# The list scheduler counts one microsecond instead of a quarter between another engine's work and the TensorE instruction that reads it

## The chip, the cores and the metric

The kernel runs on one core of a Trainium2 chip. The metric is the device time of one execution in microseconds, taken as the median of several runs. The core has five instruction streams: PE (TensorE, the matrix engine; PEld is its weight load), DVE (VectorE), ACT (ScalarE), POOL (GpSimd) and SP (SyncE, which here only issues DMAs). Each works off its own list of instructions in the order in which the program gives them; semaphores make an instruction wait for one of another engine.

## The reference

The computation is a network of four layers on 256 tokens of width 1024. The first two layers (`hybrid_layer`) normalise the residual, project it by one wide matrix, and run three branches whose results are gated and added:

```python
h = rms_norm(x, norm_w)
proj = h @ w_in                                   # 1024 -> 14352
y_a = diff_attention_branch(...)                  # 8 heads, softmax minus lambda * softmax
y_c = conformer_conv_branch(...)                  # 31-tap depthwise convolution, layer norm
y_d = gated_deltanet_branch(...)                  # chunked delta rule, triangular solve
return x + (g_a * y_a + g_c * y_c + g_d * y_d) @ w_out
```

Two more layers (`second_block`) follow. Each has a normalisation modulated by a condition vector, attention with two key/value heads, a hyena branch (a long convolution by FFT, whose filter is made by a small network of sines), a merge by gates, and a SwiGLU feed-forward part. In the third layer these run on two sequences (the 256 tokens and a context of 256); in the fourth on the tokens alone, with the context giving only keys and values. A final norm ends it. All is float32.

## The kernel before, in words

Tokens lie along the free dimension in most stages, features along the 128 partitions. A product of float32 accuracy is made of three passes: each operand is split into a high part (a copy by ACT to a narrower matmul type) and a low part (DVE subtracts the high part from the original), and `mm3` issues high times high, high times low and low times high as one unit into the same PSUM tile. Weights go the same way: `piece` lets SP load `raw` (128 x 1024 numbers, 512 KB), ACT makes `wh`, DVE makes `wl`; there are five places for `raw` and six each for `wh` and `wl`. Products of the large matrices go to three PSUM places called `gemm`; all other TensorE results share five PSUM places. Every SBUF tile called a temporary here lives in one of 54 places of 512 columns.

Between the products, DVE, ACT and POOL empty PSUM, compute softmax, convolutions, the delta rule and the splits of the activations. A norm is a chain across engines: squares on ACT, their sum on POOL or DVE (`sq`), a product with ones on PE (`ps_rms`), DVE (`rms`), a power on POOL, a diagonal matrix on DVE (`diag`), a product on PE that spreads it over the tokens (`ps_bc`), the scaled activations and their split (`h2h`, `h2l`), and only then the next products. In the third and fourth layer the hyena branch is another such chain: `vtokh` and `vtokl` (split), `ps_V` (PE), `V`, `yr` and `ys`, `Z`, `Zh` and `Zl` (split), `ps_hy` (PE). The modulation vectors (`mod_t`, 640 DVE instructions) depend on nothing but loads and are filled in wherever DVE has room.

Nothing of this is issued in program order. Every call is recorded as an `Op` (line 52) with an engine, a cost from formulas in `cost` (line 161), and edges to the operations whose results it reads or overwrites, which `touch` (line 212) finds. An edge carries a delay: `LATENCY = 0.25` us (line 42) across engines, `SAME` or nothing within one. `order` (line 329) then alternates a forward pass, a list scheduler that gives every engine the ready operation with the earliest `latest` time, and a backward pass, which works out those `latest` times from the end. It does so seven times and keeps the order whose planned span is the shortest. `emit` issues that order; the planned times themselves are thrown away. The real waits are semaphores between instructions and know nothing of the plan's delays. An operation that takes a place in SBUF or PSUM waits, in the plan, for the place to be free: that delay (lines 438 and 282) is `LATENCY` and lies outside the edges of `touch`.

An `mm3` is one operation for the plan, so that its earliest start is set by the later of its high and low operands. Since all instructions are issued from one line (472), the profile's rows are told apart by the names of their tiles.

Of the kernel before, what the change touches and what calls it, by code (L numbers as in the profile page):

```python
# [36 lines left out]
PE, DVE, ACT, POOL, DMA = range(5)  # L37
# [2 lines left out]
LATE = 0.5  # L40
HORIZON = 70.0
LATENCY = 0.25
SAME = 0.06
PASSES = 7

# [105 lines left out]
class Plan:  # L151
# [60 lines left out]
    def touch(self, op, ap, write):  # L212
        r = self.room(ap)
        if r.last is not op:
            if r.first is None:
                r.first = op
            elif r.slots:
                op.after.setdefault(r.first, -1e9)
            r.last = op
            r.touches += 1  # L220
            op.rooms.append(r)
        full = ap.full if isinstance(ap, View) else ap
        pattern = list(full.ap)
        if r.psum:
            part = (0, 1, 0, 1)
        elif full.space == DRAM:
            part = (full.offset, full.offset + 1 + sum(s * (c - 1) for s, c in pattern), 0, 1)
        else:
            p, lo = divmod(full.offset, pattern[0][0])
            part = (lo, lo + 1 + sum(s * (c - 1) for s, c in pattern[1:]), p, p + pattern[0][1])  # L230
        lo, hi, p0, p1 = part
        for wrote, accesses in ((True, r.writes), (False, r.reads)):
            if not (wrote or write):
                continue
            for o, a in accesses:
                if o is not op and a[0] < hi and lo < a[1] and a[2] < p1 and p0 < a[3]:
                    if o.engine != op.engine:
                        late = LATENCY
                    else:
                        late = SAME if wrote and not write and op.engine != PE else 0.0  # L240
                    op.after[o] = max(op.after.get(o, -1e9), late)
        if write:
            covered = lambda o, a: o is not op and lo <= a[0] and a[1] <= hi and p0 <= a[2] and a[3] <= p1
            r.writes = [x for x in r.writes if not covered(*x)]
            r.reads = [x for x in r.reads if not covered(*x)]
        (r.writes if write else r.reads).append((op, part))
# [23 lines left out]
    def backward(self, found):  # L270
# [5 lines left out]
        for op in found:  # L276
            for r in op.firsts:
                key = (id(r.slots), r.index)
                if key in last:
                    for o, _ in last[key].reads + last[key].writes:  # L280
                        if o is not op:
                            o.follow.setdefault(op, LATENCY)
                last[key] = r
# [70 lines left out]
    def forward(self):  # L354
# [28 lines left out]
        while len(found) < len(ops):  # L383
# [48 lines left out]
            for r in op.rooms:  # L432
# [3 lines left out]
                if not r.left:  # L436
                    s = r.slots
                    heappush(s.free, (op.end + LATENCY, r.index))
                    s.load[r.since:r.last.place + 1] -= 1
# [1472 lines left out]
```

## Time and profile before

| | |
|---|---|
| median of three runs | 2269.54 us (2269.27 to 2270.68) |
| the profiled execution | 2267.71 us |
| its span on the core | 2265.9 us |
| PE busy | 2222.6 us (98%), 16280 matmuls |
| DVE busy | 1912.5 us (84%) |
| ACT busy | 1114.3 us (49%) |
| POOL busy | 277.3 us (12%) |
| mean granted TensorE clock | 0.994 |

The span runs from the first to the last instruction of the program; the 1.8 us between it and the execution's time lie around it. "Busy" for PE counts the time in which at least one matmul is in the pipeline; a matmul's record lasts longer than the distance to the next one, so a waiting time shows as idle only once the pipeline has run empty.

### The profile page before, as it was taken

The page shows a single profiled execution, that of the slowest core. Times are in us where ns is not written, and L with a number is a line of the kernel's source. Part 1 is how long each engine was busy: PE and PEld are TensorE (multiplying, and loading weights), DVE is VectorE, ACT ScalarE, POOL GpSimd, SP SyncE. Part 2 cuts the span into 40 slices and gives each one's busy share as a digit, 9 for nine tenths or more (in the row PEclk, how much of TensorE's full clock was granted, in tenths as well). Part 3 has the DMA queues.
Part 4 walks back from the last instruction along what each step waited for, and adds up shares of the span by engine and source line. Part 5 has one row for each costly group of instructions (what it writes and reads, how often), then busy time and mean ns, then how long its engine had stood idle before and what let it go on. Part 6 is the DMA issues. An engine that isn't in the chain of part 4 may idle for free. (4 is left out here: it accounts for less than half of the span.)

```text
span 2265.9 us, 42914 instructions
## 1 busy us (share of the span) xinstructions
PE 2222.6 (98%) x16280; PEld 2085.7 (92%) x16280; DVE 1912.5 (84%) x4646; ACT 1114.3 (49%) x2070; POOL 277.3 (12%) x212
## 2 busy tenths in 40 slices
PE   8999999999999999999999999999999999999998
PEld 7999999999999999999889888988888898999998
DVE  8999998999999999999899988986664399867564
ACT  6556565654656665654356433332232265545443
POOL 1132110201222110111031000100000103101001
PEclk9999999999999999999999999999999999999999
DMA  7444444775545445674312566566662441555563
GB/s 267 152 150 146 129 145 161 247 242 179 168 140 142 134 143 170 232 256 139 101 57 91 155 198 206 171 203 203 212 208 77 139 145 55 170 167 196 165 197 96
DMA packets 161638, 371.14 MB, mean 164 GB/s; under 512 B 38932, under 2 KB 52500, under 8 KB 161432
## 3 DMA queue, kind: packets, MB, share of 16 engines
q1 hardware_dynamic: 161432, 368.41, 51.1%
q8 instruction: 128, 2.10, 0.4%
q14 instruction: 78, 0.64, 0.1%
HBM read 357.07 MB, written 11.28 MB: 163 GB/s over the span
## 5 line engine op out<-in xcount | busy, mean ns | idle before, releaser
L472 ACT CAST wh<-raw 128x1024 fp32r<-128x1024 f32 (+2 forms) x552 | 558.7, 1017 | 477.4 <-PE gemm L472 324.9
L472 DVE TENSOR_TENSOR wl<-raw,wh 128x1024 fp32r<-128x1024 f32 (+2 forms) x552 | 658.6, 1199 | 100.9 <-ACT wh L472 99.4
L472 PE MATMUL gemm<-hh,wh 128*128 128x256 f32 x1408 | 411.2, 292 | 0.1
L472 PE MATMUL gemm<-h2h,wh 128*128 128x256 f32 (+1 forms) x1232 | 405.1, 329 | 1.1 <-ACT h2h L472 1.1
L472 PE MATMUL gemm<-h2l,wh 128*128 128x256 f32 (+1 forms) x1232 | 401.9, 326 | 1.0 <-DVE h2l L472 0.9
L472 PE MATMUL gemm<-h2h,wl 128*128 128x256 f32 (+1 forms) x1232 | 400.8, 325 | 0.0
L472 PE MATMUL gemm<-hh,wl 128*128 128x256 f32 x1408 | 396.2, 281 | 1.4 <-DVE wl L472 1.4
L472 PE MATMUL gemm<-hl,wh 128*128 128x256 f32 x1408 | 396.5, 282 | 0.0
L472 PEld LDWEIGHTS gemm<-hh,wh 128*128 128x128 f32 x1408 | 266.5, 189 | 3.8 <-issue 2.3
L472 PEld LDWEIGHTS gemm<-hh,wl 128*128 128x128 f32 x1408 | 266.0, 189 | 2.0 <-DVE wl L472 1.8
L472 PEld LDWEIGHTS gemm<-hl,wh 128*128 128x128 f32 x1408 | 266.1, 189 | 0.1
L472 DVE CUSTOM_DVE_ANT_0 mod_t<-mod_w,mod_c 128x256 f32<-128x256 f32 x640 | 248.1, 434 | 14.1 <-DMA mod_w<-w_mod 13.8
L472 PEld LDWEIGHTS gemm<-h2h,wh 128*128 128x128 f32 x1232 | 233.0, 189 | 22.2 <-ACT h2h L472 1.2
L472 PEld LDWEIGHTS gemm<-h2l,wh 128*128 128x128 f32 x1232 | 233.1, 189 | 21.8 <-DVE h2l L472 1.6
L472 PEld LDWEIGHTS gemm<-h2h,wl 128*128 128x128 f32 x1232 | 233.3, 189 | 21.1
L472 DVE SCALAR_TENSOR_TENSOR cacc<-cu,c_conv_w,cacc 128x246 f32<-128x246 f32 (+26 forms) x480 | 228.4, 511 | 0.1
L472 POOL TENSOR_TENSOR sq<-sq 128x512 f32<-128x512 f32 (+1 forms) x39 | 56.9, 1469 | 935.9 <-ACT sq L472 934.7
L472 PE MATMUL gemm<-fh,wh 128*128 128x256 f32 (+1 forms) x374 | 123.1, 329 | 0.0
L472 PE MATMUL gemm<-fl,wh 128*128 128x256 f32 (+1 forms) x374 | 122.6, 328 | 0.0
L472 PE MATMUL gemm<-fh,wl 128*128 128x256 f32 (+1 forms) x374 | 122.5, 328 | 0.0
L472 PE MATMUL gemm<-wh,hh 128*128 128x256 f32 x320 | 93.9, 293 | 2.9 <-DVE az L472 2.4
L472 PE MATMUL gemm<-wh,h2h 128*128 128x256 f32 x320 | 93.1, 291 | 0.7 <-DVE v2l L472 0.7
(449 smaller groups left out, 5035.4 us busy)
## 6 DMA issues: line engine op xcount, KB each, us to landing
raw<-w_in SPq DMA_DIRECT2D x296, 512.0 KB, 3.7
mod_w<-w_mod SPq DMA_DIRECT2D x192, 256.0 KB, 3.5
raw<-w_gate_up SPq DMA_DIRECT2D x88, 512.0 KB, 3.7
raw<-w_out SPq DMA_DIRECT2D x32, 512.0 KB, 4.4
raw<-w_down SPq DMA_DIRECT2D x32, 384.0 KB, 3.2
raw<-w_down SPq DMA_DIRECT2D x32, 320.0 KB, 2.9
raw<-w_attn_out SPq DMA_DIRECT2D x16, 512.0 KB, 4.4
raw<-w_dn_out SPq DMA_DIRECT2D x16, 512.0 KB, 3.5
```

The costliest lines, as they stand in the source:

```text
L472: call(*map(real, args), **{k: real(x) for k, x in kw.items()})
```

## The change

Edges that lead from another engine's operation to a TensorE operation get a delay of 1.0 us in the plan instead of 0.25. This holds wherever `touch` makes the edge, so for every matmul, transpose and `mm3` that reads what DVE, ACT, POOL or a DMA wrote, and in both passes. Edges from PE to other engines, among other engines, and the turns of places in SBUF and PSUM keep 0.25. No instruction is added, removed or changed; which order each engine's list is in, and which of the free places a tile gets, is worked out anew.

```diff
 LATENCY = 0.25
+MARGIN = 1.0
 SAME = 0.06
...
                     if o.engine != op.engine:
-                        late = LATENCY
+
+                        late = MARGIN if op.engine == PE else LATENCY
                     else:
                         late = SAME if wrote and not write and op.engine != PE else 0.0
                     op.after[o] = max(op.after.get(o, -1e9), late)
```

## Rows read from the trace of the kernel before

**Rows 1.** The page's first part: busy time, share of the span, instructions.

```profile
PE 2222.6 (98%) x16280; PEld 2085.7 (92%) x16280; DVE 1912.5 (84%) x4646; ACT 1114.3 (49%) x2070; POOL 277.3 (12%) x212
```

**Rows 2.** Stretches: length, each engine's busy time (instructions), granted clock, DMA share, GB/s.

```profile
0.00:50.00 50.00, 38.84 (x304) 38.07 (x305) 41.76 (x99) 32.94 (x53) 8.62 (x15) 1.00 0.81 273
...
700.00:750.00 50.00, 47.18 (x397) 45.55 (x397) 48.30 (x120) 30.36 (x66) 16.64 (x12) 1.00 0.42 120
2000.00:2050.00 50.00, 50.00 (x425) 50.00 (x424) 30.31 (x38) 23.13 (x27) 0.00 (x0) 1.00 0.54 179
2250.00:2265.90 15.90, 6.46 (x52) 6.02 (x50) 3.97 (x9) 3.65 (x8) 4.01 (x4) 0.78 0.19 66
```

**Rows 3.** PE's waits: who waited for whom, us, times, longest.

```profile
PE gemm L472 <- ACT w4h L472: 7.1, 1, 7.1
PE gemm L472 <- DVE w4l L472: 4.1, 2, 2.5
PE ps_hy L472 <- DVE Zl L472: 3.1, 3, 1.9
PE ps_V L472 <- DVE vtokl L472: 3.1, 2, 2.4
PE gemm L472 <- DVE wl L472: 2.9, 4, 1.2
PE gemm L472 <- DVE az L472: 2.4, 2, 2.1
PE ps_rms L472 <- POOL sq L472: 2.3, 2, 1.5
PE ps_rms L472 <- DVE sq L472: 1.9, 2, 1.0
PE ps_bc L472 <- DVE diag L472: 1.5, 2, 1.4
PE ps_kk L472 <- DVE dk L472: 1.3, 1, 1.3
PE gemm L472 <- ACT h2h L472: 1.1, 1, 1.1
PE gemm L472 <- DVE h2l L472: 0.9, 2, 0.6
PE ps_rms L472 <- ACT sq L472: 0.7, 2, 0.5
PE gemm L472 <- DVE v2l L472: 0.7, 1, 0.7
PE gemm L472 <- DVE cu L472: 0.5, 1, 0.5
```

**Rows 4.** PE's timeline around the longest wait of the middle.

```profile
1153.62 0.39 PE L472 MATMUL ps_V<-vtokh,dfth 128*128 128x512 f32 x1
1156.40 0.79 PE L472 MATMUL ps_V<-vtokl,dfth 128*128 128x512 f32 x1 [2.40 <-DVE vtokl L472]
...
1160.60 0.28 PE L472 MATMUL gemm<-wh,h2h 128*128 128x256 f32 x1
```

**Rows 5.** DVE's timeline in the same stretch.

```profile
1154.53 1.21 DVE L472 TENSOR_TENSOR wl<-raw,wh 128x1024 fp32r<-128x1024 f32 x1
1155.67 1.27 DVE L472 TENSOR_TENSOR vtokl<-ps_vtok,vtokh 128x512 fp32r<-128x512 f32 x2
```

**Rows 6.** The middle's four stretches of low granted clock, columns as in rows 2.

```profile
1023.20:1033.40 10.20, 9.20 (x43) 9.20 (x44) 10.13 (x31) 4.82 (x12) 3.33 (x2) 0.50 0.58 158
1156.30:1159.70 3.40, 3.30 (x8) 2.62 (x9) 3.26 (x9) 0.99 (x2) 1.01 (x1) 0.51 0.64 204
1903.90:1907.30 3.40, 3.40 (x15) 3.11 (x15) 3.40 (x10) 0.61 (x2) 2.26 (x2) 0.50 0.00 0
2064.30:2067.70 3.40, 3.40 (x19) 3.40 (x18) 1.71 (x3) 1.04 (x1) 1.36 (x2) 0.50 0.70 255
```

**Rows 7.** The norms' chains: one row of the view of the tile ps_rms.

```profile
L472 DVE TENSOR_SCALAR rms<-ps_rms x12: 145/152/160, 18.1 to 2256.5; 128x2 f32<-128x2 f32 x12
```

## The prediction, made before the changed kernel was run

> **What bounds the kernel now.** I read the page's busy shares first, then busy time by stretches, then PE's waits, then the timelines on both sides of the longest waits, then the clock.
>
> PE is busy 2222.6 of 2265.9 us [rows 1]; 43.3 us of the span are idle PE. In a stretch of nothing but products of 256 columns PE does 425 matmuls in 50 us, 0.118 us each, with no idle time at all [rows 2]. No change of order makes that faster, so what can be won is idle time and the clock lost beside it. The first stretch of 50 us has 11.2 us of idle PE and the last 15.9 us have 9.4 [rows 2]: at the start PE waits for the first loads and their split, at the end for the last norm and the stores. In both nothing else is there to be done. That leaves 43.3 - 20.6 = 22.7 us in the middle.
>
> The waits of PE by releaser tell what these are [rows 3]. The view has 32 waits with 35.3 us in all; behind `cu` four rows of one wait each are left out (`p`, `a_sm` and `hn_y` with 0.5 us each, `d_r` with 0.2). The start's are `w4h` and `w4l` (11.2 us), the end's are `ACT sq` (0.7) and the longest one of `diag` (1.4). The remainder is 22.0 us in 26 waits, which agrees with the 22.7.
>
> They are of two kinds. `az`, `cu` and `v2l` empty a `gemm` place of PSUM: a product waited for the place, 3.6 us in 4 waits. The plan's delay for that isn't touched. The other 22 waits, 18.4 us, are for an operand made by DVE, ACT or POOL: the kind that the change is about. Nearly all are DVE's. DVE was not idle then but busy with other things: before the longest one PE issued the first product of `vtokh` at 1153.62 and got `vtokl` only for 1156.40, while DVE did a `wl` at 1154.53 and began the two `vtokl` at 1155.67 [rows 4, 5]. Products whose operands need nothing of this stood behind in PE's list (`gemm` at 1160.60). In 700 to 750 us DVE is busy 48.3 of 50 us and PE loses 2.8 [rows 2]: the order there is a matter of tenths of a microsecond on both engines.
>
> The second loss is the clock. In four stretches of the middle the granted clock is 0.5, 1.2 in place of 2.4 GHz, 20.4 us in all [rows 6]. Three begin during or just after waits (two for `POOL sq`, 2.3 us together; `vtokl` 2.4; `Zl` 1.9), the fourth without a listed wait. Fully at work, a slow stretch loses half its length: 5.1 us for the long one, 1.7 for each short one.
>
> **The change, part by part.** It adds, removes and resizes no instruction; so the direct cost is nothing, and each engine's busy time stays. Everything comes by way of the order.
>
> *PE's order.* In the plan a matmul may now start 0.75 us later after its operand than before. Where another product is ready, the scheduler puts it first. On the chip that is six products of 0.118 us between the time at which the plan takes the operand as done and the time at which PE comes to it. The semaphore wait itself is no longer: an operand that comes late by less than 0.75 us is then met without idle time, one that comes later stalls PE 0.75 us less. So a wait can lose at most its own length or 0.75 us. Row by row of the operand waits, the lesser of the row's sum and 0.75 us times its count: `Zl` 2.25, `vtokl` 1.5, `wl` 2.9, `POOL sq` 1.5, `DVE sq` 1.5, `diag` 0.1 (the one of the middle), `dk` 0.75, `h2h` 0.75, `h2l` 0.9, `p`, `a_sm` and `hn_y` 1.5, `d_r` 0.2: 13.85 us [rows 3].
>
> Of this `POOL sq` (1.5) and `h2h` (0.75) I take as nothing: they lie where one layer's norm ends and the next layer's first products need it, and there is no other product to put in between. 11.6 us are left. I take two thirds, 7.7 us. Not all, since a plan that is worked out anew brings new close meetings elsewhere; not a third, since six products' room is more than most of these waits are long (18.4 us by 22 is 0.84 us in the mean). The bounds are 0 and 18.4 us, the latter where DVE's order changes as well.
>
> *The producers' order.* The backward pass counts the same delay, so whatever feeds PE is due 0.75 us earlier. On DVE and ACT it passes by what doesn't (`mod_t`, the convolutions). The `wl` ahead of `vtokl` [rows 5] feeds PE as well, so among those two nothing changes. What empties PSUM falls back by 0.75 us against a `wl`; waits of that kind are 3.6 us now. A `wl` of 1.21 us ahead of such an instruction costs PE at most that, and with three `gemm` places mostly nothing. I take zero for this part, between -3 us (three of the longest waits end one `wl` earlier) and +3.6 (the waits for places double).
>
> *The chains.* Where PE waits in the plan anyway, the plan now shows 0.75 us of room before PE's step, and the next step on DVE or ACT is planned 0.75 us later. Into that room the scheduler can put a filler, which on the chip then delays the real step. There are 12 chains of norms [rows 7] and the double one at the seam to the third layer, 13 in all, with three steps into PE each (`ps_rms`, `ps_bc`, the first product): 39 steps. Cover is the rest of PE's work: it hides a later step wherever products are ready. It is missing where PE already waits with nothing else to do: `POOL sq` twice and `h2h` once [rows 3]. I count 3 x 0.75 = 2.25 us of loss there; the bounds are 0 and 39 x 0.75 = 29.3 us.
>
> *The clock.* Of the short slow stretches behind `vtokl` and `Zl` I count one as gone, 1.7 us: their waits of 2.4 and 1.9 us get shorter by 0.75 at most, not to nothing. The bounds are 8.5 us won (5.1 + 2 x 1.7) and as much lost, if new waits do the same elsewhere. The Trainium skill ("TensorE: Matmul & The Clock Gate", section "Why this matters for your kernels") says that idle gaps of PE between bursts of matmuls send it back to the slow clock. By that, ending the gaps would give back all three stretches; the fourth of them here stands after one-column products and no listed wait [rows 6], so the rule doesn't tell all.
>
> *Sum.* -7.7 + 0 + 2.25 - 1.7 = -7.15 us. The profiled execution took 2267.71 us (span 2265.9 and 1.8 around it), so 2260.6; the median of the runs stands 1.83 us above it, so the prediction is 2262.4, rounded 2262.
>
> **The rivals.**
>
> A. *The waits only move.* Where DVE is nearly full [rows 2], PE must wait somewhere for what DVE hasn't done; after each stall PE meets DVE with the new order's next close spot. For it: DVE busy 48.3 of 50 us while PE loses 2.8. Against it: most of the waiting time (`Zl`, `vtokl`, `sq`, `h2h`) lies in stretches where ready products stand behind. It gives between no change and a third of 11.6 us: about 2268. The Trainium skill ("Perfetto Trace Analysis", section "Optimization Strategy") has one find the gaps of the most contended engine and make the dependencies that end them start sooner or complete faster. This change does neither by itself; by that reading it stays at 2269.5.
>
> B. *The chains stretch, and it is slower.* Fillers get into the room before half of the 39 steps: 19.5 x 0.75 = 14.6 us, against 7.7 + 1.7 won: +5.2 us, 2275. It decides from 13 paid steps on (9.4 / 0.75 = 12.5), and from 19 on it is slower by more than can be told from no change. For it: the norm of the seam to the third layer already stalls PE twice within 3 us and costs 10.2 us of slow clock [rows 3, 6]. Against it: outside of five waits of norms PE has work at all of them.
>
> C. *Stalls and slow clock go together.* The order on DVE improves too, 13.85 us of waits and the two short slow stretches (3.4) go, and 2.25 for the uncovered steps stay: -15.0 us, and with the seam's slow stretch gone (-5.1) -20.1: 2249 to 2255.
>
> **How the numbers follow.** A measurement of this kernel can tell about 0.2%, 4.5 us, from no change. The forecast (2255 to 2265) has 0.43, A (2265 to 2274) 0.25, B (above 2274) 0.22, C (below 2255) 0.10. Faster is the forecast and C, 0.53; slower is B; the same is A. The range for 8 in 10 runs from 2250, which takes in most of C, to 2277, a little beyond B's middle; that leaves out a few hundredths of C and half of B. The likeliest case's own range is 2255 to 2265.
>
> **What would show it.** Right: the same counts and durations of every group; PE's waits of the middle for operands at 11 us or less in place of 18.4, above all `wl`, `DVE sq`, `Zl` and `vtokl` shorter; the waits for `az`, `cu`, `v2l` about as now; one slow stretch of the clock fewer; start and end unchanged within 1 us. A would show equal idle time under other names. B would show waits of `ps_rms`, `ps_bc`, `h2h`, `ps_V` and `ps_hy` longer, with DVE or ACT doing something unrelated just before. C would show a mean clock of 0.998 or more. The prediction is wrong if the order changes so much (another of the seven passes kept, places of SBUF taken otherwise) that the rows of before say little of the stalls of after.

## The result and the profile after

The changed kernel is slower: 2284.8 us (2282.95 to 2285.27, four runs) against 2269.4 us (2268.29 to 2270.68), a ratio of 1.0065 with a 95% interval of 1.0053 to 1.0077. The forecast was 2262 with a range up to 2277, so the sign is wrong and the range is missed by 8 us. Executions of one kernel differ too: the seven of margin_024, the widest below, lie between 2272.93 and 2283.51. The profiled execution took 2282.95 us with a span of 2280.9, which is 15.0 more than before.

The page's first part, in the columns of [rows 1], for the changed kernel:

```profile
PE 2229.4 (98%) x16280; PEld 2090.7 (92%) x16280; DVE 1919.6 (84%) x4646; ACT 1117.6 (49%) x2072; POOL 289.4 (13%) x212
```

The work is the same: the same counts on PE, DVE and POOL. PE's idle time rose from 43.3 us [rows 1] to 2280.9 - 2229.4 = 51.5. The stretches that answer to [rows 2], the third one 15 us later:

```profile
0.00:50.00 50.00, 39.53 (x306) 38.87 (x307) 40.66 (x100) 34.48 (x54) 9.78 (x15) 1.00 0.80 275
...
2015.00:2065.00 50.00, 50.00 (x424) 50.00 (x424) 30.08 (x38) 23.47 (x29) 0.00 (x0) 1.00 0.54 177
2265.00:2280.90 15.90, 6.95 (x52) 6.40 (x50) 3.98 (x9) 3.65 (x8) 4.00 (x4) 0.75 0.19 66
```

Start and end are as before within 1 us (10.5 and 9.0 us of idle PE against 11.2 and 9.4), and the stretch of mere products is still full. The loss is in the middle. PE's waits by releaser, as in [rows 3]:

```profile
PE gemm L474 <- ACT w4h L474: 7.1, 1, 7.1
PE ps_hy L474 <- DVE Zl L474: 5.0, 3, 2.8
PE gemm L474 <- DVE wl L474: 4.8, 4, 2.7
PE gemm L474 <- ACT h2h L474: 4.0, 3, 2.1
PE gemm L474 <- DVE h2l L474: 3.5, 4, 1.4
...
PE ps_rms L474 <- POOL sq L474: 2.8, 2, 1.8
PE ps_mean L474 <- POOL ln_s L474: 1.7, 2, 1.1
PE ps_bc L474 <- DVE diag L474: 1.6, 2, 1.4
...
PE ps_hyt L474 <- DVE vtokl L474: 0.8, 1, 0.8
```

With the rows left out the view has 39 waits of 44.3 us in all; before it had 32 of 35.3. Without the start (`w4h`, `w4l`, 10.5) and the end (`ACT sq` and the longest of `diag`, 2.1), and without the waits for a PSUM place (`az`, `cu`, `qk_y`, 2.0 together), 30 waits of 29.7 us for an operand remain, where 22 of 18.4 us stood before. `vtokl`, `dk` and `DVE sq` did shrink, by 4.9 us together. `Zl` and `wl` grew by 3.8, `h2h` and `h2l` by 5.5 (2.0 to 7.5), and names that had no wait before (`ln_s`, `ro_a`, `gpl`, `ycl`, `d_S` and three smaller ones) brought 7.0.

The stretches of the middle at the lower granted clock, in the columns of [rows 6]:

```profile
279.50:282.90 3.40, 3.40 (x21) 3.06 (x20) 1.65 (x4) 0.02 (x1) 0.00 (x0) 0.50 0.53 166
655.00:658.40 3.40, 3.40 (x18) 3.40 (x17) 3.40 (x6) 1.94 (x3) 0.00 (x0) 0.50 0.33 94
740.30:743.70 3.40, 3.40 (x19) 3.40 (x18) 3.40 (x10) 0.77 (x2) 3.33 (x3) 0.50 0.47 157
1033.90:1044.10 10.20, 10.20 (x48) 10.20 (x49) 4.66 (x22) 1.46 (x4) 1.51 (x2) 0.50 0.71 220
1832.60:1839.40 6.80, 5.96 (x26) 5.66 (x27) 6.80 (x18) 3.54 (x8) 0.00 (x0) 0.50 0.22 73
2085.20:2088.60 3.40, 3.32 (x15) 3.32 (x16) 3.40 (x10) 2.01 (x5) 0.00 (x0) 0.50 0.47 184
```

That is 30.6 us at 1.2 GHz where 20.4 stood before [rows 6]; at half speed it costs 5.1 us more. That is an upper figure: in the stretch at 1832.6 the products stand 0.21 us apart in place of 0.12, by which 10.2 us cost 4.6. The account of the 15.0: operand waits +11.3, waits for places -1.6, start -0.7, clock +5.1, together 14.1; 0.9 is not assigned (1.4 with the smaller figure).

**Where along the run.** The tile views give the first and last start of a stage's products. Of the changed kernel, for the merge of the first two layers (`mh`), that of the last two (`m2h`) and the feed-forward output (`fh`):

```profile
L474 PE MATMUL gemm<-mh,wh x128: 277/282/365, 496.6 to 1027.7; 128*128 128x256 f32 x128
L474 PE MATMUL gemm<-m2h,wh x160: 276/282/402, 1409.2 to 2071.2; 128*128 128x256 f32 x128, 128*128 128x512 f32 x32
L474 PE MATMUL gemm<-fh,wh x374: 274/283/401, 1594.4 to 2268.5; 128*128 128x256 f32 x110, 128*128 128x512 f32 x77
```

And of the kernel before:

```profile
L472 PE MATMUL gemm<-mh,wh x128: 277/282/288, 490.8 to 1020.0; 128*128 128x256 f32 x128
L472 PE MATMUL gemm<-m2h,wh x160: 274/282/398, 1403.3 to 2057.5; 128*128 128x256 f32 x128, 128*128 128x512 f32 x32
L472 PE MATMUL gemm<-fh,wh x374: 274/283/401, 1584.8 to 2253.5; 128*128 128x256 f32 x110, 128*128 128x512 f32 x77
```

By the last `mh` product, the end of the second layer, the new order is 1027.7 - 1020.0 = 7.7 us late; I call this the head. From the first `m2h` product (merge of the third layer) to the last `fh` product (end of the fourth) it takes 859.3 us against 850.2: 9.1 more, the tail. Between the two it wins 1.8. Of the tail's 9.1, the waits for `h2h` and `h2l` (2.0 to 7.5, all of them at three norms there) are 5.5 and the clock 1.7 (slow stretches of 10.2 us where 6.8 stood); 1.9 is not assigned.

**What happened in the tail.** PE's timeline at the norm ahead of the fourth layer, before (18 `fh` and `fl` products and `ps_f` between its rows are left out):

```profile
1817.82 0.61 PE L472 MATMUL ps_bc<-diag,ones 128*128 128x128 f32 x4
...
1821.16 0.28 PE L472 MATMUL gemm<-h2h,wh 128*128 128x256 f32 x1
```

After:

```profile
1829.62 0.28 PE L474 MATMUL gemm<-fh,wl 128*128 128x256 f32 x1
1829.73 0.60 PE L474 MATMUL ps_bc<-diag,ones 128*128 128x128 f32 x4
1830.27 0.64 PE L474 MATMUL ps_f<-f_h,c_f_w 64*64 64x256 f32 x2
1832.54 0.58 PE L474 MATMUL gemm<-h2h,wh 128*128 128x256 f32 x1 [1.62 <-ACT h2h L474]
1833.96 0.58 PE L474 MATMUL gemm<-h2l,wh 128*128 128x256 f32 x1 [0.84 <-DVE h2l L474]
```

And DVE in the same stretch, after:

```profile
1827.73 0.48 DVE L474 TENSOR_SCALAR diag<-c_ident,rms 128x128 f32<-128x128 f32 x2
...
1830.34 1.22 DVE L474 TENSOR_TENSOR wl<-raw,wh 128x1024 fp32r<-128x1024 f32 x1
1831.47 2.04 DVE L474 SCALAR_TENSOR_TENSOR h<-xres,modvFalse,ps_bc 128x256 f32<-128x256 f32 x5
```

In the kernel before, DVE in that stretch:

```profile
1817.34 0.48 DVE L472 TENSOR_SCALAR diag<-c_ident,rms 128x128 f32<-128x128 f32 x2 [0.60 <-POOL rms L472]
...
1817.94 1.21 DVE L472 TENSOR_TENSOR wl<-raw,wh 128x1024 fp32r<-128x1024 f32 x1
1819.07 1.64 DVE L472 SCALAR_TENSOR_TENSOR h<-xres,modvFalse,ps_bc 128x256 f32<-128x256 f32 x4
```

Read them together. After, `diag` is done at 1828.2, but PE first takes 13 more ready products and comes to `ps_bc` at 1829.73. Before, `ps_bc` followed `diag` at once, and 18 ready products stood *behind* it: these covered the 3.3 us in which DVE and ACT made `h2h`, although DVE put a `wl` in front of `h` then too. Now all of them stand *ahead* of `ps_bc`, behind it only two small `ps_f` are left to do, and the same `wl` is no longer hidden. PE waits 1.62 and 0.84, together 2.46 us, and from 1832.6 works at 1.2 GHz for 6.8. I call the ready products between the first `ps_bc` and the first `h2h` product the cover. At the feed-forward norm of the fourth layer the cover went from 9 products to none in the same way; here the `wl` ahead of `h` is new. The wait there went from 1.13 us to 2.74; before, then after:

```profile
2070.76 0.38 PE L472 MATMUL gemm<-h2h,wh 128*128 128x256 f32 x1 [1.13 <-ACT h2h L472]
```

```profile
2084.25 0.38 PE L474 MATMUL gemm<-h2h,wh 128*128 128x256 f32 x1 [2.09 <-ACT h2h L474]
2085.28 0.58 PE L474 MATMUL gemm<-h2l,wh 128*128 128x256 f32 x1 [0.65 <-DVE h2l L474]
```

At the third norm of the tail, the feed-forward norm of the third layer, the cover only shrank, from 30 products to 21, and the waits rose from 0.6 us to 2.3.

### The profile page after: what moved, and what is told of

Its sections match the earlier page's. It is cut to its first block, busy times and chain, and to the rows that moved or that the text cites. A ratio compares the mean times of both kernels' runs of the same rounds, so it can differ in the third digit from the quotient of the medians.

```text
span 2280.9 us, 42952 instructions
## 1 busy us (share of the span) xinstructions
PE 2229.4 (98%) x16280; PEld 2090.7 (92%) x16280; DVE 1919.6 (84%) x4646; ACT 1117.6 (49%) x2072; POOL 289.4 (13%) x212
## 5 line engine op out<-in xcount | busy, mean ns | idle before, releaser
L474 DVE CUSTOM_DVE_ANT_0 mod_t<-mod_w,mod_c 128x256 f32<-128x256 f32 x640 | 248.6, 432 | 12.8 <-DMA mod_w<-w_mod 12.1
L474 DVE SCALAR_TENSOR_TENSOR cacc<-cu,c_conv_w,cacc 128x235 f32<-128x235 f32 (+28 forms) x480 | 228.6, 516 | 0.0
```

Of the source, the lines that this page charges most:

```text
L474: call(*map(real, args), **{k: real(x) for k, x in kw.items()})
```

## The experiments

All are the changed kernel with one edit, so only the order differs; every kernel computes the whole. Two theories were to be told apart: that the longer delay on operands itself does the harm, at the norms above all, or that any new order of this scheduler costs about as much. Where an expectation speaks of "up to 997 us" and "behind 1443 us", it reads head and tail at the first `mh` product of the second layer and near the end of the third layer's `m2h`; that differs from the marks above by at most 2.0 us. The table has all runs. Clock is the time lost to the lower clock, over the three stages, summed from the granted clock in stretches of 3 us. Cover is given for the norm ahead of the fourth layer and for its feed-forward norm, counted in PE's timeline. Each ratio is to executions of the kernel before that were taken beside the run (medians 2269.4 to 2270.4). The order, and with it the cover, is the same in every execution of a kernel; head, tail, waits and clock are of the one execution that was profiled, so differences of a few microseconds between two rows show little by themselves.

| kernel | us | ratio to before, 95% | head | tail | waits `h2h`+`h2l` | cover | clock |
|---|---|---|---|---|---|---|---|
| before | 2269.4 | 1 | 0 | 0 | 2.0 | 18, 9 | 10.2 |
| after (1.0 us) | 2284.8 | 1.0065, 1.0053 to 1.0077 | +7.7 | +9.1 | 7.5 | 0, 0 | 15.3 |
| margin_024 | 2280.96 | 1.0038, 1.0024 to 1.0052 | +8.9 | +3.0 | 1.9 | 18, 9 | 25.6 |
| margin_026 | 2273.75 | 1.0019, 1.0011 to 1.0028 | +9.3 | -0.9 | 2.2 | 18, 9 | 13.6 |
| same_055 | 2277.21 | 1.0032, 1.0020 to 1.0044 | +10.0 | +1.3 | 2.7 | 15, 9 | 17.0 |
| same_065 | 2268.85 | 0.9996, 0.9987 to 1.0006 | +2.0 | +0.2 | 2.0 | 18, 9 | 11.9 |
| horizon_72 | 2276.84 | 1.0029, 1.0018 to 1.0040 | +7.4 | +2.7 | 1.9 | 18, 9 | 18.7 |
| weights_only | 2275.64 | 1.0027, 1.0017 to 1.0036 | +2.6 | +1.0 | 1.9 | 18, 9 | 10.2 |
| weights_095 | 2283.07 | 1.0055, 1.0039 to 1.0072 | +12.1 | +4.6 | 1.9 | 18, 9 | 13.6 |
| chains_only | 2280.64 | 1.0043, 1.0028 to 1.0058 | +9.5 | +5.6 | 6.8 | 0, 0 | 11.9 |
| chains_095 | 2280.79 | 1.0041, 1.0026 to 1.0056 | +12.1 | +3.8 | 3.9 | 0, 0 | 15.3 |
| norms_only | 2288.05 | 1.0074, 1.0062 to 1.0087 | +15.5 | +3.5 | 5.5 | 3, 0 | 8.5 |
| norms_quarter | 2280.25 | 1.0048, 1.0034 to 1.0062 | +14.0 | +0.3 | 2.5 | 18, 0 | 10.2 |
| diag_quarter | 2282.49 | 1.0050, 1.0030 to 1.0070 | +16.4 | +3.0 | 3.3 | 0, 12 | 18.7 |
| h2_quarter | 2276.29 | 1.0026, 1.0016 to 1.0037 | +9.4 | +7.7 | 5.9 | 0, 0 | 18.7 |
| margin_050 | 2274.79 | 1.0025, 1.0015 to 1.0034 | +8.2 | +8.0 | 6.0 | 0, 6 | 15.3 |
| margin_095 | 2279.81 | 1.0050, 1.0035 to 1.0065 | +20.8 | +3.0 | 3.7 | 0, 0 | 23.9 |
| margin_200 | 2307.47 | 1.0161, 1.0144 to 1.0178 | +26.5 | +17.5 | 11.7 | 0, 0 | 27.3 |

**Orders drawn anew.** Five kernels hardly change the delay, or leave it at 0.25 and move another constant of the plan by a little, so that the scheduler comes to another order for a reason that has next to nothing to do with operands of PE.

```diff
-MARGIN = 1.0
+MARGIN = 0.26
```

> The change with a delay of 0.26 us in place of 1.0: next to no margin, but a plan worked out from other numbers. 'Cover used up': no loss that has to do with the delay, ratio 0.998 to 1.002. 'New draw': it may lie as far off as the change itself, 0.994 to 1.008, which then is the size of the draw.

```diff
-MARGIN = 1.0
+MARGIN = 0.24
```

> The change with a delay of 0.24 us, a hundredth less than before. 'New draw' (the order before was a better than usual one, and any other set of numbers falls back): slower than before by 0.1 to 0.6%, most of it in the first two layers, like the 0.26 us (ratio 1.0019). 'Cover used up' alone: no loss, 0.999 to 1.001.

```diff
-HORIZON = 70.0
+HORIZON = 72.0
 LATENCY = 0.25
-MARGIN = 1.0
+MARGIN = 0.25
```

In same_065 and same_055 `HORIZON` stays 70.0, `MARGIN` is 0.25 as well, and `SAME` is 0.065 or 0.055 in place of 0.06.

> All delays 0.25 us as before; of the scheduler, the stretch in which buffers are given out ahead is 72 us in place of 70, which means nothing for the order of single steps but sets it anew. 'New draw': slower than before by 0.1 to 0.5%, in the first two layers (4 us or more up to 997 us of the kernel before), and next to nothing behind 1443 us. 'Change alone' (the loss of the first layers belongs to the longer delay): 0.999 to 1.001, as before.

> All delays across engines 0.25 us as before; the delay within one engine is 0.065 us in place of 0.06. The same bet as the one before: 'new draw' 1.001 to 1.005 with the loss in the first two layers, 'change alone' 0.999 to 1.001.

> All delays across engines 0.25 us, the delay within one engine 0.055 us in place of 0.06: a fifth order without a longer delay. Both theories: 0 to 9 us lost up to 997 us, 3 us or less behind 1443 us, ratio 0.999 to 1.004.

They give 0.9996, 1.0019, 1.0029, 1.0032 and 1.0038, in the mean 1.0023, about 5 us. That is within what 'new draw' had expected of all but same_065 (1.001 to 1.005). None is faster than the kernel before beyond the interval; its order is a better draw than four of these and equal to the fifth. Most of the loss is in the head (+2.0 to +10.0 us). The tail stays between -0.9 and +3.0, the waits for `h2h` and `h2l` at 1.9 to 2.7 us, and the cover at 15 or 18 and 9. So the changed kernel's +7.7 in the head is nothing that a new order alone doesn't give; its +9.1 in the tail, and the lost cover, are beyond all five.

**The delay's size.**

```diff
-MARGIN = 1.0
+MARGIN = 0.5     # 0.95 in margin_095, 2.0 in margin_200
```

> Delay 0.5 us. 'Cover used up': a third of the way from 0.26 to 1.0, ratio 1.002 to 1.004, waits for h2h and h2l of 3 to 5 us. 'New draw': no order in the delays, 0.998 to 1.010.

> Delay 0.95 us, for all that the delay means the same as 1.0. 'Cover used up': the loss behind the norms of the third and fourth layer (8.6 us between 1443 us of the kernel before and the end) is there again, 6 us or more, and the whole ratio 1.005 to 1.008. 'New draw': that part of the loss is as likely to be gone, ratio 0.998 to 1.010.

> Delay 2.0 us. 'Cover used up': the loss grows with the delay, over 12 us from 1443 us on, waits for h2h and h2l of 8 us or more, ratio 1.008 to 1.015; the waits for wl go under 1 us. 'New draw': no more than the others, 1.001 to 1.008.

At 0.5 us the tail loses 8.0 us already (in the slowest of that kernel's ten executions), at 2.0 us 17.5, with the cover of the norm ahead of the fourth layer gone in all. The waits for `h2h` and `h2l`, expected at 3 to 5 us for 0.5, are 6.0. The waits for `wl`, expected under 1 us at 2.0, are 3.1. With 0.95 us the tail lost 3.0 only: a miss for a loss that grows with the delay. DVE's timeline at that norm tells why, of margin_095:

```profile
1836.03 0.88 DVE L474 SCALAR_TENSOR_TENSOR xres<-gemm,modvTrue,xres 128x256 f32<-128x256 f32 x2 [1.71 <-PE gemm L474]
1836.83 1.65 DVE L474 SCALAR_TENSOR_TENSOR h<-xres,modvFalse,ps_bc 128x256 f32<-128x256 f32 x4
```

The first row ends a wait of DVE of 1.71 us; no `wl` stands between `ps_bc` (issued at 1835.83) and `h`. PE's wait for `h2h` is 1.01 us in place of 1.62. The longest delay is the other end; PE, of margin_200, and then DVE:

```profile
1852.08 0.71 PE L474 MATMUL ps_bc<-diag,ones 128*128 128x128 f32 x4
1856.19 0.38 PE L474 MATMUL gemm<-h2h,wh 128*128 128x256 f32 x1 [3.40 <-ACT h2h L474]
```

```profile
1852.41 1.22 DVE L474 TENSOR_TENSOR wl<-raw,wh 128x1024 fp32r<-128x1024 f32 x1
...
1854.00 1.21 DVE L474 TENSOR_TENSOR wl<-raw,wh 128x1024 fp32r<-128x1024 f32 x1
1855.13 1.64 DVE L474 SCALAR_TENSOR_TENSOR h<-xres,modvFalse,ps_bc 128x256 f32<-128x256 f32 x4
```

Two `wl` ahead of `h`, and 3.40 us. With no cover the wait for `h2h` at this norm is thus 1.0 us without a filler (the same in chains_095 and diag_quarter), 1.6 with one `wl` behind `ps_bc` (the same in margin_050 and chains_only) and 3.4 with two. The fillers fall in front of `h` or not by the draw, so the loss of one such kernel is no clean function of the delay. With cover a `wl` at the same place costs nothing: the kernel before and norms_quarter, below, have one too and don't wait for `h2h` there.

**Weights alone, and all but the weights.**

```diff
-                        late = MARGIN if op.engine == PE else LATENCY
+                        late = MARGIN if op.engine == PE and r.name in ("wh", "wl") else LATENCY
```

> The delay of 1.0 us on the split weights wh and wl alone; all chains keep 0.25. 'Cover used up': chains are not set back, so no loss at the norms, and the waits for wl (2.9 us before, 4.8 after the change) go down to 1 or 2: ratio 0.997 to 1.001. A third theory, 'weights crowd out chains' (weights get due 0.75 us earlier on DVE, so a wl of 1.2 us goes ahead of the chain's step, as at 1830 us in the changed kernel): waits for h2h and h2l of 6 us or more here too, ratio 1.003 to 1.007. 'New draw': 0.994 to 1.010.

The same with `MARGIN = 0.95`:

> 0.95 us on wh and wl alone, 0.25 on the rest. 'The delay costs on the chains only': up to 997 us it loses what an order drawn anew loses, 0 to 9 us (1.0 us on the weights lost 2.6), behind 1443 us nothing; ratio 0.999 to 1.004, waits for wl under 1 us. 'The draw alone': the same. 'Any longer delay costs': 10 us or more up to 997 us.

```diff
-                        late = MARGIN if op.engine == PE else LATENCY
+                        late = MARGIN if op.engine == PE and r.name not in ("wh", "wl") else LATENCY
```

> 1.0 us on everything but wh and wl. 'The delay costs on the chains only': 10 us or more lost up to 997 us and 3 us or more behind 1443 us, ratio 1.005 to 1.012. 'The draw alone': 0 to 9 us up to 997 us, and behind it as the change, ratio 1.002 to 1.008.

The same with `MARGIN = 0.95`:

> 0.95 us on everything but wh and wl: the same bets as for 1.0 us, drawn once more.

With the delay on the weights alone there is little waiting for `wl`: 2.9 us before, no row of that name in weights_only, 0.5 in weights_095. That the delay does this isn't shown: same_055, without a longer delay, has 0.2, and the changed kernel and norms_quarter, with 1.0 us on the weights, have 4.8 and 4.4. The cover stays (18, 9). But neither is faster. weights_only was expected at 1.001 at most if only the chains cost, weights_095 at 1.004 at most under both theories; both are above. PE's waits in weights_only show where it waits instead; the first rows without those of the start:

```profile
PE ps_hy L474 <- DVE Zl L474: 4.6, 3, 2.3
PE ps_vn L474 <- DVE d_r L474: 3.2, 4, 2.0
...
PE ps_kk L474 <- DVE dk L474: 2.8, 3, 1.0
```

`d_r` had 0.2 us before and `dk` 1.3 [rows 3], and all waits of this kernel sum to 38.6 us against 35.3. The wait stands under other names; its sum is no more than in the five draws (34.0 to 39.1). The two weights kernels differ by 0.05 us of delay and by 9.5 us in the head, which looks like a difference of draws; weights_095 alone would fit 'any longer delay costs' (10 us or more), weights_only with +2.6 speaks against it. With the delay on all but the weights the cover is gone (0, 0) and the waits for `h2h` and `h2l` are 6.8 and 3.9 us. So the lost cover and the waits behind it come by the chains, not by the weights. The tail's time doesn't part the two as cleanly: weights_095 loses 4.6 there with the cover whole, 3.4 of it by slow stretches of the clock, chains_095 3.8. The ratios of chains_only and chains_095 lie below the 1.005 that was expected if the chains alone cost.

**The norms' edges.** The names of the steps of a norm, and of the `gph` and `gpl` split, are taken out of the longer delay, or get it alone:

```diff
-                        late = MARGIN if op.engine == PE else LATENCY
+                        late = MARGIN if op.engine == PE and r.name not in ("sq", "ln_s", "diag", "h2h", "h2l", "hh", "hl", "gph", "gpl") else LATENCY
```

> The change, but the operands of the norm chains (sq, ln_s, diag, and the activations h2h, h2l, hh, hl, gph, gpl that come out of a norm) keep the delay of 0.25 us. Theory 'cover used up' (with the longer delay PE takes the ready products ahead of the norm's own step, and has none left for the wait behind it): the waits for h2h and h2l, 7.5 us after the change against 2.0 before, go back to about 2, the slow stretch of 6.8 us at 1832 us goes, and some 9 of the 15 us come back: ratio to the kernel before 1.001 to 1.004. Theory 'new draw' (any small shift of the plan throws the order of the close meetings anew): the ratio is anywhere from 0.996 to 1.010, and the waits come back under other names.

The same list with `in` for `not in`:

> The kernel before, with 1.0 us on the operands of the norm chains alone. 'Cover used up': the loss of these chains stands here by itself, waits for h2h and h2l of 6 us or more, ratio 1.003 to 1.006. 'New draw': no tie between the edges that got the longer delay and the waits that grow; ratio anywhere from 0.996 to 1.010.

With the nine names back at 0.25 the tail is at +0.3 and the waits for `h2h` and `h2l` at 2.5 us. PE of norms_quarter, the 18 products after `ps_bc` and the one of `ps_f` left out:

```profile
1829.40 0.60 PE L474 MATMUL ps_bc<-diag,ones 128*128 128x128 f32 x4
...
1832.61 0.38 PE L474 MATMUL gemm<-h2h,wh 128*128 128x256 f32 x1
```

The cover is there again, and no wait for `h2h`. The ratio, 1.0048, misses the 1.001 to 1.004 that was expected, by the head. Two things limit this reading. The feed-forward norm of the fourth layer still has no cover in this kernel; it waits less because no `wl` stands ahead of `h` (0.44 us for `h2h` in place of 2.09). And it has no slow stretch of the clock in the tail, where the kernel before loses 3.4 us; without that luck its tail would be at about +3.7. The delay on the nine names alone brings the waits (5.5 us) and takes the cover (3, 0), though the tail is only 3.5 longer; expected were 6 us or more of waits and a ratio of at most 1.006. The head is worse in both (+14.0, +15.5) than in the five draws (at most +10.0), with the delay on these names and with it off them.

**Which step of the norm.**

```diff
-                        late = MARGIN if op.engine == PE else LATENCY
+                        late = MARGIN if op.engine == PE and r.name not in ("sq", "ln_s", "diag") else LATENCY
```

> The change, with 0.25 us on what feeds the small products of a norm alone (sq, ln_s, diag); h2h, h2l and the other activations keep 1.0. 'Cover used up' puts the loss at the step of ps_bc, which PE comes to only behind the last ready products: with that step early again the waits for h2h and h2l are 3 us or less and the part behind 1443 us loses 3 us at most (8.6 in the change). If the loss sits at the activations, that part loses 6 us or more. The first two layers: a draw, 4 to 14 us lost.

The same with `("h2h", "h2l")`:

> The change, with 0.25 us on h2h and h2l alone; sq, ln_s and diag keep 1.0. 'Cover used up' at ps_bc: waits for h2h and h2l stay at 5 us or more, the part behind 1443 us loses 5 us or more. If the loss sits at the activations: 3 us or less for both. The first two layers: a draw, 4 to 14 us lost.

Taking the delay off the last step alone changes nothing: tail +7.7, waits 5.9, cover 0, 0. Taking it off the small steps alone (`sq`, `ln_s`, `diag`) brings the waits to 3.3 and the tail to +3.0, but by the timelines this is half a cure: 12 products of `gph` cover the feed-forward norm again, while ahead of the fourth layer the cover is still 0, with 1.01 us for `h2h` since no `wl` stands ahead of `h`. No single step holds the effect.

**Cover, stall and clock over all kernels.** Nine of the kernels have 0 to 3 products of cover at the norm ahead of the fourth layer, and there PE waits 1.0 to 3.4 us for `h2h`; the other nine, the kernel before among them, have 15 or 18 and don't wait for `h2h` there. In seven of the first nine (not in margin_050 and norms_only) a slow stretch of the clock begins within 3 us behind that stall, at 1832.6 in the changed kernel; in none of the second nine is there one at this norm.

## Why the prediction was wrong

**"PE's order", -7.7: the step that failed.** It was to take 7.7 us off 18.4 us of operand waits; they rose by 11.3 instead. Two things were wrong in it. I counted what the delay does to the waits that the old order had, row by row, as if the rest stayed. Of the rows counted, `vtokl`, `DVE sq` and `dk` shrank, and `Zl`, `wl`, `h2h` and `h2l` grew; 7.0 us came under new names. The prediction's last line names this premise as what could make it wrong, but gave it no price; five neutral orders price it at about +5 us in the mean, for the whole time. The sentence "where another product is ready, the scheduler puts it first" is the second. It is what happened, and at a norm it is the harm: the product put first is the one that would have covered the next step of the same chain. Where a wait did go, as for `wl` in weights_only, nothing was gained: PE waits no less in sum (38.6 us against 35.3). That part is rival A.

**"The chains", +2.25: mis-sized, and by the wrong count.** I charged three steps where PE had nothing else to do and said that "cover is the rest of PE's work", as if it were fixed. The order decides where cover stands. Of the three waits that it took as bare, the one for `h2h` (the feed-forward norm of the fourth layer) had nine products behind `ps_bc`, which the new order used up. At the three norms of the tail (the third layer's feed-forward norm and the two above) the waits went from 2.0 to 7.5 us, all of the waits for `h2h` and `h2l` in [rows 3] and after: 5.5 us where 2.25 was set. The tail as a whole paid 9.1.

**"The clock", -1.7.** One slow stretch fewer was forecast; six stand where four did, +5.1 us. The longest new one begins with the stall at the norm and is missing in all nine kernels that don't wait for `h2h` there, so I take it as a follower of the failed step. The other new ones aren't traced to a cause. The Trainium skill ("TensorE: Matmul & The Clock Gate", section "Why this matters for your kernels") warns of idle gaps between bursts of matmuls. The trace agrees in the direction only, since that section means longer gaps than any wait of the middle here: its slow stretch at 1832.6 stands right behind a wait of 1.62 us.

**Rival B** had the right sign and the right chain, and half of the mechanism. Fillers on DVE ahead of the real step are there, though at the norm ahead of the fourth layer the kernel before had one as well: one `wl` costs 0.6 us at one norm (1.62 against 1.01) and 1.65 at the other (2.09 against 0.44, with DVE's wait for `wh` in it). But at that norm they cost only where PE's cover is gone, which B didn't have; and B's time, 2275, lacks the clock and the head. Of the names it gave, `h2h` and `ps_hy` wait longer, `ps_bc` as before, `ps_rms` and `ps_V` less.

**What held.** Counts and work unchanged; start and end within 1 us; waits for PSUM places not longer (3.6 to 2.0 us), so the "producers' order" at nothing is not contradicted. The Trainium skill ("Perfetto Trace Analysis", section "Optimization Strategy") has one make the dependencies that end a gap start sooner or complete faster; this change did neither, and the gaps grew.

**What stays open.** Why the plan drops the cover isn't shown. Two steps of 0.75 us would put about 13 products ahead (1.5 / 0.118), and 12 were (33 in place of 21 between `ps_rms` and `ps_bc`); but at 0.5 us, with two steps of 0.25, it drops all 18 too. The planned times would tell and leave no trace on the chip. The +7.7 us of the head can't be told from a new draw. Seven other kernels have heads of +12.1 to +26.5, beyond the five draws, but apart from the 2.0 us at the upper end I found no pattern in them: 0.95 us costs 20.8 where 1.0 costs 7.7. In the mean the twelve kernels with a longer delay on some edges lose 12.9 us in the head, the five draws 7.5, so that a longer delay may cost there too; no run shows by what. No order found here beats the kernel before; same_065 equals it.

## What to carry to other kernels

Slack that a list scheduler is told to leave ahead of a matmul can be filled with ready matmuls, as it was here, and these may be the cover of the next step of the same chain; look behind the small matmul of a chain for what is left to do, not only at the wait ahead of it. Before a scheduler's constant is judged, draw a few orders with changes that mean nothing: here they alone cost up to 0.38%, more than half of the effect that was to be explained. And a row-by-row account of old waits prices a change of the order only if most of the order stays.

## What was not expected of the hardware

Some instructions of DVE take nearly twice their usual time. In the changed kernel PE's longest wait for `wl`, 2.66 us, ends with such a one; DVE's timeline, then POOL's:

```profile
215.44 1.21 DVE L474 TENSOR_TENSOR wl<-raw,wh 128x1024 fp32r<-128x1024 f32 x1
216.57 3.66 DVE L474 SCALAR_TENSOR_TENSOR cacc<-cu,c_conv_w,cacc 128x226 f32<-128x226 f32 x4
220.16 2.28 DVE L474 TENSOR_TENSOR wl<-raw,wh 128x1024 fp32r<-128x1024 f32 x1
222.36 0.45 DVE L474 SCALAR_TENSOR_TENSOR cacc<-cu,c_conv_w,cacc 128x235 f32<-128x235 f32 x1
```

```profile
216.99 2.98 POOL L474 TENSOR_TENSOR d_M<-d_Lo,c_masks 128x512 f32<-128x512 f32 x2 [3.96 <-ACT d_Lo L474]
219.94 1.42 POOL L474 TENSOR_TENSOR d_S<-c_masks,d_E 128x512 f32<-128x512 f32 x1
```

The `wl` of 2.28 us, and four `cacc` of 0.9 us each where the one behind the `wl` has 0.45, lie beside POOL's work from 216.99 to 221.36; the `wl` of 1.21 lies just ahead of it. The whole trace bears this out. Of the 488 `wl` of this shape in the changed kernel, 401 have no POOL work beside them and take 1.18 to 1.23 us each; 87 have some, and 11 of these take over 1.5 us, up to 2.32. In all 11 a POOL instruction had begun ahead of the `wl` and still ran. No kernel was run to show that POOL is the cause. If it is, an order also sets durations, which the plan's costs don't know.
